# Tanh for the compression MLP's activation, and a strict alternation of MLP tiles with gate half blocks on TensorE

## The chip, the cores and the metric

The kernel runs on one core of a Trainium2 chip. The metric is the device time of one execution in microseconds (us). The engines are named as the profile names them: PE is TensorE (matmul), PEld its weight load, DVE VectorE, ACT ScalarE, POOL GpSimd, SP the engine that here only issues DMAs.

## The reference

One decoder layer over 1024 tokens of 1024 channels, in float32. What matters here is the token compression of its sparse attention branch, and the gate paths:

```
def compress_blocks(t, pe, w1, w2):      # overlapping blocks of 32 tokens, stride 16: 63 blocks
    blk = t[:, :, idx] + pe
    flat = blk.reshape(B, G, nc, CMP_BLOCK * dh)          # 2048 values a block
    return jax.nn.silu(flat @ w1) @ w2                    # hidden 256, out 64
...
proj = h @ w_in[l]                       # q, k, v, z_a, z_b, merge ... are columns of it
kc = compress_blocks(kc_raw, pe_k, w_cmp_k1, w_cmp_k2)
vc = compress_blocks(vc_raw, pe_v, w_cmp_v1, w_cmp_v2)
...
y_a = (merge_heads(o_a) * jax.nn.silu(z_a)) @ w_o_nsa
y_b = (merge_heads(o_b) * jax.nn.silu(z_b)) @ w_o_swa
```

`silu(u)` is `u / (1 + exp(-u))`, which is also `0.5 * u * (1 + tanh(u / 2))`.

## The kernel before, in words

A float32 product is formed as three passes of TensorE over operands split into a high part (a rounded cast) and a low part (operand minus high part): high times high, low times high, high times low. Every weight therefore goes through four steps: a DMA into `wraw` (SP's queue), a cast to `wh` (ACT, for the first two blocks of this stage DVE, L175), a subtraction to `wl` (POOL, L182), and then the matmuls.

The program has a prologue (norms, value and key projections, up to about 92 us), the stage that is changed here (about 92 to 192 us), the attention, and the output projections. In the changed stage three streams are interleaved:

- **The gate half blocks.** `z_steps` (L573) projects six blocks of gate columns, ZB0 to ZB3, ZA0 and ZA1. A block has two token halves of 24 matmuls of 512 columns (L580, L583, L584), and is a generator that yields after each 12: 24 steps in all, each called by `z_step`. The result leaves a bank of PSUM (`b_s` and `b_pj` in turn) in `z_out`: a tanh on ACT (L569), a multiplication on DVE (L570), a store.
- **The two MLPs.** `blocks_of(side)` copies the raw keys or values into overlapping blocks `flat` with four copies on ACT (L705, the key-block copies for side 0) and adds the position embedding on DVE (L706). `mlp(side)` splits `flat` into `fh` (ACT, L714) and `fl` (DVE, L715), and walks over eight tiles of the first weight matrix, each with a load to `w1raw` (ACT's queue), a cast (ACT, L722), a subtraction (DVE, L723) and six matmuls of 256 columns (L726, L729, L730). Then come the activation (`he`, L735 to L738), two transposes on PE (L741), the copy `h1T` (L743), and the second matrix (L749 or L760).
- **Side work hung on the gate steps.** `gate_sum` loads 16 rows `gr` of the modulation weights (ACT's queue, L670, two buffers) and reduces each on DVE (L672). `input_sums` forms sums of the normed input on POOL (L634, L637). When the last `gr` is reduced, the same buffer takes the distance table `DC`, which the first attention scores need (L925).

The order on each engine is made by a scheduler that follows priorities and the extra orderings given by `after(ins, other)`, which add no wait of their own, only a place in the order. Each engine then runs its list strictly in order; an instruction that waits holds up everything behind it. `last["act"]` and `last["dve"]` are the ACT and the DVE instruction of the last query block of the prologue (`q_block`, L522 and L523). `z_done[-1]` is the last matmul of the newest gate step.

Before, the tiles of an MLP are ordered behind gate steps only in part (L727), the gate steps are not ordered behind MLP tiles at all, and no gate step is called between the end of `mlp(0)` and the second tile of `mlp(1)`.

Of the kernel before, what the change touches and what calls it, by code (L numbers as in the profile page):

```python
# [7 lines left out]
F32 = mybir.dt.float32  # L8
F32R = mybir.dt.float32r
AF = mybir.ActivationFunctionType  # L10
ALU = mybir.AluOpType
# [3 lines left out]
P = 128  # L15
# [55 lines left out]
def hybrid_kernel(tc, io, out):  # L71
# [97 lines left out]
    def split_half(raw, shape, low=None):  # L169
        wh = wp.tile(shape, F32R, name="wh", tag="wh", bufs=WBUFS)  # L170
        wl = wp.tile(shape, F32R, name="wl", tag="wl", bufs=WBUFS)
        if low is None and hold[0] is None and not ended:
            cast_count[0] += 1
            if cast_count[0] < 3:
                after(ins := nc.vector.tensor_copy(wh, raw), last["dve"])  # L175
            else:
                after(ins := nc.scalar.copy(wh, raw), last["act"])
        else:
            ins = nc.scalar.copy(wh, raw)  # L179
        chain("wh", ins)  # L180
        if low is None:
            chain("wl", nc.gpsimd.tensor_tensor(wl, raw, wh.bitcast(F32), ALU.subtract))  # L182
        else:
            act(ins)
            low.append(lambda: chain("wl", dve(nc.vector.tensor_tensor(wl, raw, wh.bitcast(F32), ALU.subtract))))
        return wh, wl
# [386 lines left out]
    def z_steps(names):  # L573
        w = load_block(names[0])
        for n, name in enumerate(names):
            for half in range(2):
                t = bank(("s", "pj")[z_count[0] % 2])
                for kc in range(KC):
                    wh, wl = (x[:, kc % KH, :] for x in w[kc // KH])
                    ins = nc.tensor.matmul(t, lhsT=wh, rhs=hh[kc][half], start=(kc == 0), stop=False)  # L580
                    if kc == 0:
                        chain("pj", ins)
                    nc.tensor.matmul(t, lhsT=wh, rhs=hl[kc][half], start=False, stop=False)  # L583
                    ins = nc.tensor.matmul(t, lhsT=wl, rhs=hh[kc][half], start=False, stop=(kc == KC - 1))  # L584
                    if kc == 3:
                        yield ins
                z_out(name, half, t)
                if half == 0 and n + 1 < len(names):
                    following = load_block(names[n + 1])
                yield ins  # L590
            w = following
# [91 lines left out]
    with tc.tile_pool(name="c1", bufs=1, reuse_waits="tile") as c1:  # L683
# [12 lines left out]
        def blocks_of(side):  # L696
            raw = raws[side]
            pe = sm.tile([P, 16], F32, name="pe", tag="pe", bufs=2)
            after(nc.scalar.dma_start(pe, io["peT"][side]), last["act"])
            flat = c1.tile([P, 16, P], F32, name="flat", tag="flat", bufs=1)  # L700
            nc.gpsimd.memset(flat[:, :, 126:], 0.0)
            for g in range(2):
                rg = raw[64 * g : 64 * g + 64]
                for j in range(2):
                    nc.scalar.copy(flat[64 * j : 64 * j + 64, :, 63 * g : 63 * g + 63], rg[:, :, j : j + 63])  # L705
            nc.vector.tensor_tensor(  # L706
                flat[:, :, :126], flat[:, :, :126], pe.unsqueeze(2).broadcast_to([P, 16, 126]), ALU.add)
            flats.append(flat)

        def mlp(side):  # L710
            flat = flats[side]
            fh = c1.tile([P, 16, P], F32R, name="fh", tag="fh", bufs=1)
            fl = c1.tile([P, 16, P], F32R, name="fl", tag="fl", bufs=1)
            nc.scalar.copy(fh, flat)  # L714
            nc.vector.tensor_tensor(fl, flat, fh.bitcast(F32), ALU.subtract)  # L715
            t = bank("pt")
            for n in range(8):
                raw = c1.tile([P, HS], F32, name="w1raw", tag="w1raw", bufs=3)
                chain("w1raw", nc.scalar.dma_start(raw, io["w1"][side, n]))

                w1h, w1l = (kq.tile([P, P + HS], F32R, name="w1", tag="kts", bufs=8)[:, :HS] for _ in range(2))
                chain("kts", nc.scalar.copy(w1h, raw))  # L722
                nc.vector.tensor_tensor(w1l, raw, w1h.bitcast(F32), ALU.subtract)  # L723
                for l in (2 * n, 2 * n + 1):
                    h, lo = (x[:, l % 2 * 256 : l % 2 * 256 + 256] for x in (w1h, w1l))
                    ins = nc.tensor.matmul(t[:, :256], lhsT=fh[:, l, :], rhs=h, start=(l == 0), stop=False)  # L726
                    if n and (side == 0 or n % 2 == 0) and l == 2 * n:  # L727
                        after(ins, z_done[-1])
                    nc.tensor.matmul(t[:, :256], lhsT=fh[:, l, :], rhs=lo, start=False, stop=False)  # L729
                    nc.tensor.matmul(t[:, :256], lhsT=fl[:, l, :], rhs=h, start=False, stop=(l == 15))  # L730
                if (side == 0 or n % 2) and n < 7:
                    with tc.high_priority(offset=-500):
                        z_step()
            he = c1.tile([P, 256], F32, name="he", tag="he", bufs=1)
            nc.scalar.activation(he[:126], t[:126, :256], AF.Exp, scale=-1.0)  # L735
            nc.vector.tensor_scalar(he[:126], he[:126], 1.0, None, ALU.add)
            nc.vector.reciprocal(he[:126], he[:126])
            nc.vector.tensor_tensor(he[:126], t[:126, :256], he[:126], ALU.mult)  # L738
            t = bank("pt")
            for k in range(2):  # L740
                nc.tensor.transpose(t[:, k * P : k * P + 126], he[:126, k * P : k * P + P], ident[:126, :126])  # L741
            h1T = c1.tile([P, 2, 126], F32, name="h1T", tag="h1T", bufs=1)
            nc.vector.tensor_copy(h1T, t[:, :256].rearrange("p (k r) -> p k r", k=2)[:, :, :126])  # L743
            t = bank("pt")
            if side == 0:
                w2 = c1.tile([P, 2, P], F32, name="w2k", tag="w2")
                nc.scalar.dma_start(w2, io["w2k"])
                for k in range(2):
                    nc.tensor.matmul(t[:, :126], lhsT=w2[:, k, :], rhs=h1T[:, k, :], start=(k == 0), stop=(k == 1))  # L749
                kcf = c1.tile([P, 2, 64], F32, name="kcf", tag="cf", bufs=2)  # L750
                nc.vector.memset(kcf, 0.0)
                nc.vector.tensor_copy(kcf[:, :, :63], t[:, :126].rearrange("p (g c) -> p g c", g=2))
                nc.vector.tensor_copy(kc2[:, 0], kcf)
                nc.vector.tensor_tensor(kc2[:, 1], kcf, kc2[:, 0].bitcast(F32), ALU.subtract)
            else:
                w2 = c1.tile([P, 2, 64], F32, name="w2v", tag="w2")
                nc.scalar.dma_start(w2, io["w2v"])
                for g in range(2):
                    for k in range(2):
                        nc.tensor.matmul(  # L760
                            t[:63, g * 64 : g * 64 + 64], lhsT=h1T[:, k, 63 * g : 63 * g + 63], rhs=w2[:, k, :],
                            start=(k == 0), stop=(k == 1))

                for par in range(2):
# [5 lines left out]
                    nc.vector.tensor_tensor(vc2[:, par, :, 1, :], vcf, vc2[:, par, :, 0, :].bitcast(F32), ALU.subtract)  # L770


        zs = z_steps([f"Z{m}{b}" for m, b in (("B", 0), ("B", 1), ("B", 2), ("B", 3), ("A", 0), ("A", 1))])
        for _ in range(3):
            z_step()
        with tc.high_priority(offset=500):
            blocks_of(0)
            mlp(0)
            blocks_of(1)
            mlp(1)  # L780
        while len(z_done) < 24:
            z_step()
        for n in sorted(z_work):
# [1006 lines left out]
```

## Time and profile before

| what | value |
|---|---|
| time, median of 3 runs | 893.46 us (892.33 to 894.55) |
| the profiled execution: time, span | 894.23 us, 892.4 us |
| mean granted TensorE clock | 0.992 |
| busy share of the span: PE, PEld, DVE, ACT, POOL | 97%, 82%, 69%, 60%, 59% |
| chain that ended last | PE through the output stage, then a tail on DVE, ACT and POOL |
| window 92 to 192 us: PE busy, granted clock | 88.05 us of 100, 0.95 |
| window 192 to 250 us: PE busy, granted clock | 58.00 us of 58, 1.00 |

The span runs from the first to the last instruction; the time of the execution is about 2 us longer. A matmul of 512 columns shows a length of about 0.39 us, but matmuls overlap: what counts for the length of a stretch is the distance of their starts. An idle time in square brackets is that of the engine just before the instruction, with what released it.

### The profile page before, as it was taken

The page shows a single profiled execution, that of the slowest core. Times are in us where ns is not written, and L with a number is a line of the kernel's source. Part 1 is how long each engine was busy: PE and PEld are TensorE (multiplying, and loading weights), DVE is VectorE, ACT ScalarE, POOL GpSimd, SP SyncE. Part 2 cuts the span into 40 slices and gives each one's busy share as a digit, 9 for nine tenths or more (in the row PEclk, how much of TensorE's full clock was granted, in tenths as well). Part 3 has the DMA queues.
Part 4 walks back from the last instruction along what each step waited for, and adds up shares of the span by engine and source line. Part 5 has one row for each costly group of instructions (what it writes and reads, how often), then busy time and mean ns, then how long its engine had stood idle before and what let it go on. Part 6 is the DMA issues. An engine that isn't in the chain of part 4 may idle for free. (4 is left out here: it accounts for less than half of the span.)

```text
span 892.4 us, 14782 instructions
## 1 busy us (share of the span) xinstructions
PE 868.3 (97%) x4418; PEld 731.9 (82%) x4418; DVE 619.0 (69%) x1587; ACT 536.2 (60%) x1220; POOL 530.3 (59%) x547
## 2 busy tenths in 40 slices
PE   9999897999999999999999999999999999999996
PEld 7889686778888888888888888888888788877885
DVE  5866756456666677766766577777676399778996
ACT  6566732247777787766656797666665475444341
POOL 1000674467878787888535597765656379645541
PEclk9999999999999999999999999999999999999998
DMA  9975495585555535474324243343363599841333
GB/s 351 308 254 155 149 313 196 158 262 177 171 145 161 154 114 180 160 242 137 91 83 144 73 133 119 113 124 107 122 192 126 158 338 300 283 129 48 107 97 116
DMA packets 93298, 151.47 MB, mean 170 GB/s; under 512 B 10913, under 2 KB 28705, under 8 KB 93218
## 3 DMA queue, kind: packets, MB, share of 16 engines
q1 hardware_dynamic: 87168, 140.38, 48.2%
q10 hardware_dynamic: 6050, 10.14, 3.9%
q8 instruction: 35, 0.57, 0.3%
q14 instruction: 45, 0.37, 0.1%
HBM read 108.81 MB, written 38.01 MB: 165 GB/s over the span
## 5 line engine op out<-in xcount | busy, mean ns | idle before, releaser
L182 POOL TENSOR_TENSOR wl<-wraw,wh 128x512 fp32r<-128x512 f32 x123 | 164.3, 1339 | 110.6 <-ACT wh L179 66.7
L991 DVE TENSOR_TENSOR pl<-b_pt,ph 128x512 fp32r<-128x512 f32 x162 | 110.7, 687 | 39.1 <-ACT ph L990 38.2
L990 ACT CAST ph<-b_pt 128x512 fp32r<-128x512 f32 x162 | 93.5, 584 | 55.6 <-PE b_pt L984 46.6
L938 ACT ACTIVATE ps<-ps,mins 128x257 f32<-128x257 f32 (+9 forms) x128 | 81.3, 636 | 37.3 <-DVE mins L925 29.9
L179 ACT CAST wh<-wraw 128x512 fp32r<-128x512 f32 x115 | 70.6, 618 | 54.3 <-PE b_pj L1063 18.0
L915 PE MATMUL b_s<-kh,q 128*128 128x256 f32 (+6 forms) x272 | 86.0, 322 | 2.1 <-DVE sp L570 1.6
L918 PE MATMUL b_s<-kl,q 128*128 128x256 f32 (+6 forms) x272 | 83.5, 314 | 0.0
L947 POOL TENSOR_SCALAR ps<-ps,rr,gates 128x128 f32<-128x128 f32 (+7 forms) x64 | 52.4, 822 | 50.5 <-DVE rr L942 31.6
L1058 PE MATMUL b_pj<-hh,wh 128*128 128x512 f32 x188 | 77.4, 412 | 0.0
L1064 PE MATMUL b_pj<-hh,wl 128*128 128x512 f32 x188 | 74.0, 394 | 0.0
L1063 PE MATMUL b_pj<-hl,wh 128*128 128x512 f32 x188 | 74.0, 394 | 0.0
L995 PE MATMUL b_pv<-pl,V 128*128 128x512 f32 x162 | 68.3, 422 | 1.2 <-DVE pl L991 0.9
L984 PE MATMUL b_pt<-ident,ps 128*128 128x128 f32 x408 | 67.1, 272 | 0.0
L992 PE MATMUL b_pv<-ph,V 128*128 128x512 f32 x162 | 66.7, 412 | 0.1
L915 PEld LDWEIGHTS b_s<-kh,q 128*128 128x128 f32 x272 | 51.2, 188 | 9.9 <-DVE sp L570 1.8
L984 PEld LDWEIGHTS b_pt<-ident,ps 128*128 128x128 f32 x408 | 51.0, 140 | 9.2
L947 POOL TENSOR_SCALAR pw<-pw,rr,gates 128x640 f32<-128x640 f32 (+4 forms) x64 | 47.3, 742 | 17.9 <-DVE rr L942 10.8
L918 PEld LDWEIGHTS b_s<-kl,q 128*128 128x128 f32 x272 | 51.2, 189 | 7.2
L938 ACT ACTIVATE pw<-pw,mins 128x640 f32<-128x640 f32 (+4 forms) x64 | 44.5, 696 | 11.9 <-DVE mins L925 11.0
L942 DVE RECIPROCAL rr<-sums 128x1 f32<-128x1 f32 x192 | 28.2, 159 | 28.1 <-ACT pw L938 13.3
L925 DVE CUSTOM_DVE_ANT_0 ps<-b_s,DC 128x512 f32<-128x512 f32 (+3 forms) x64 | 35.0, 553 | 13.8 <-PE b_pt L984 10.2
L205 PE MATMUL b_pj<-hh,wh 128*128 128x512 f32 x112 | 44.5, 397 | 0.0
(463 smaller groups left out, 2581.1 us busy)
## 6 DMA issues: line engine op xcount, KB each, us to landing
wraw<-in_w_blk SPq DMA_DIRECT2D x83, 256.0 KB, 3.2
r<-in_w_out SPq DMA_DIRECT2D x32, 256.0 KB, 4.8
wa<-in_w_adaT SPq DMA_DIRECT2D x15, 512.0 KB, 4.6
wraw<-sS SPq DMA_DIRECT2D x28, 256.0 KB, 2.8
w1raw<-in_w ACTq DMA_DIRECT2D x16, 256.0 KB, 2.7
gr<-in_w_adaT ACTq DMA_DIRECT2D x16, 256.0 KB, 4.3
wraw<-in_w_o SPq DMA_DIRECT2D x16, 256.0 KB, 4.3
t<-od SPq DMA_DIRECT2D x16, 256.0 KB, 4.7
```

Of the source, the lines that this page charges most:

```text
L179: ins = nc.scalar.copy(wh, raw)
L182: chain("wl", nc.gpsimd.tensor_tensor(wl, raw, wh.bitcast(F32), ALU.subtract))
L915: ins = nc.tensor.matmul(sp[:, :n_in], lhsT=q, rhs=rh, start=True, stop=False)
L918: nc.tensor.matmul(sp[:, :n_in], lhsT=q, rhs=rl, start=False, stop=True)
L938: nc.scalar.activation(rows[r][:, :on], rows[r][:, :on], AF.Exp, scale=-1.0, bias=last_min[:, r : r + 1], accum_out=sums[:, r : r + 1])
L947: nc.gpsimd.tensor_scalar(rows[r][:, :off], rows[r][:, :off], rr[:, r : r + 1], gate, ALU.mult, ALU.mult)
L984: ins = nc.tensor.transpose(t[:, r * P : r * P + P], rows[r][:, off : off + P], ident)
L990: nc.scalar.copy(ph, t)
L991: nc.vector.tensor_tensor(pl, t, ph.bitcast(F32), ALU.subtract)
L1058: ins = nc.tensor.matmul(self.t, lhsT=wh[:, kc, :], rhs=hi, start=(self.first is None and kc == 0), stop=False)
L1063: nc.tensor.matmul(self.t, lhsT=wh[:, kc, :], rhs=lo, start=False, stop=False)
L1064: ins = nc.tensor.matmul(self.t, lhsT=wl[:, kc, :], rhs=hi, start=False, stop=(kc == KH - 1 and self.stop))
```

## The change

1. The activation of the MLP is `tanh(u/2)` on ACT and one `(tanh + 1) * u` on DVE, in place of exp on ACT and add, reciprocal and multiply on DVE. The factor 0.5 is taken with the copy `h1T`, which becomes a multiplication.
2. Every MLP tile is ordered behind the newest gate step, and every gate step (12 matmuls) behind the newest MLP tile and the gate half before it. A gate step is called behind each of the 16 tiles, and one more behind each MLP's activation.
3. The end of an MLP (transposes, `h1T`, second matrix) becomes a generator of two parts. That of side 0 runs behind the second and third tile of side 1; that of side 1 behind two more gate steps.
4. The four block copies and the position's addition are ordered behind the last query's instruction on ACT (`last["act"]`) and behind DVE's first two weight casts (`last["cast"]`, which later is the activation of the first MLP). The second side's blocks are called within the first MLP (behind its third tile).
5. `fh` and `fl` are formed in two halves.

```diff
@@ split_half
             if cast_count[0] < 3:
                 after(ins := nc.vector.tensor_copy(wh, raw), last["dve"])
+                last["cast"] = ins
@@ z_steps
+                    if kc in (0, 4):
+                        for earlier in ("mlp", "z"):
+                            if earlier in last:
+                                after(ins, last[earlier])
...
+                last["z"] = ins
                 z_out(name, half, t)
@@ blocks_of
-                    nc.scalar.copy(flat[...], rg[:, :, j : j + 63])
-            nc.vector.tensor_tensor(flat..., pe..., ALU.add)
+                    ins = nc.scalar.copy(flat[...], rg[:, :, j : j + 63])
+                    after(ins, last["act"])
+            ins = nc.vector.tensor_tensor(flat..., pe..., ALU.add)
+            after(ins, last["cast"])
@@ mlp
-            nc.scalar.copy(fh, flat)
-            nc.vector.tensor_tensor(fl, flat, fh.bitcast(F32), ALU.subtract)
+            for part in (slice(0, 8), slice(8, 16)):
+                nc.scalar.copy(fh[:, part], flat[:, part])
+                ins = nc.vector.tensor_tensor(fl[:, part], flat[:, part], fh[:, part].bitcast(F32), ALU.subtract)
+                after(ins, last["cast"])
...
-                    if n and (side == 0 or n % 2 == 0) and l == 2 * n:
+                    if l == 2 * n:
                         after(ins, z_done[-1])
...
-                if (side == 0 or n % 2) and n < 7:
-                    with tc.high_priority(offset=-500):
-                        z_step()
+                if side == 0 and n == 2:
+                    blocks_of(1)
+                if side and n in (1, 2):
+                    next(ends_[0])
+                with tc.high_priority(offset=-500):
+                    z_step()
...
-            nc.scalar.activation(he[:126], t[:126, :256], AF.Exp, scale=-1.0)
-            nc.vector.tensor_scalar(he[:126], he[:126], 1.0, None, ALU.add)
-            nc.vector.reciprocal(he[:126], he[:126])
-            nc.vector.tensor_tensor(he[:126], t[:126, :256], he[:126], ALU.mult)
+            nc.scalar.activation(he[:126], t[:126, :256], AF.Tanh, scale=0.5)
+            last["cast"] = nc.vector.scalar_tensor_tensor(he[:126], he[:126], 1.0, t[:126, :256], ALU.add, ALU.mult)
+            with tc.high_priority(offset=-500):
+                z_step()
+            ends_.append(mlp_end(side, he))
...
-            nc.vector.tensor_copy(h1T, t[:, :256]...)
+            nc.vector.tensor_scalar(h1T, t[:, :256]..., 0.5, None, ALU.mult)
+            yield
@@ the calls
             blocks_of(0)
             mlp(0)
-            blocks_of(1)
             mlp(1)
+            next(ends_[1])
+        z_step()
+        next(ends_[1])
         while len(z_done) < 24:
             z_step()
```

How this moves instructions is seen in the order on each engine. Line numbers behind the change are larger: L705 becomes L711, L522 becomes L523, L714 becomes L723, L741 becomes L758, L735 becomes L749, L580 becomes L581.

First, ACT where the prologue ends (`w` is a part of an MLP weight tile, `q` the last query, `flat` the blocks, `gates` and `cg` side work). Before:

```order
L722 CAST w_1248<-w1raw 128x512
L705 COPY flat<-craw 64x16x63 x4
L522 ACTIVATE q<-b_pt 64x512
L699 DMA pe<-in_peT 128x16
L719 DMA w1raw<-in_w 128x512
L699 DMA pe<-in_peT 128x16
L719 DMA w1raw<-in_w 128x512
L270 ACT_TABLE_LOAD
L270 ACTIVATE gates<-gates 128x96 x2
L690 COPY craw<-b_s 128x16x32
L177 CAST wh<-wraw 128x512
L714 CAST fh<-flat 128x2048
```

And now:

```order
L732 CAST w_1259<-w1raw 128x512
L523 ACTIVATE q<-b_pt 64x512
L705 DMA pe<-in_peT 128x16
L711 COPY flat<-craw 64x16x63 x4
L705 DMA pe<-in_peT 128x16
L729 DMA w1raw<-in_w 128x512 x2
L271 ACT_TABLE_LOAD
L271 ACTIVATE gates<-gates 128x96 x2
L178 CAST wh<-wraw 128x512
L696 COPY craw<-b_s 128x16x32
L663 DMA cg<-in_c 128x512
L676 DMA gr<-in_w_adaT 128x512
```

The query now stands ahead of the four copies, and `fh` (its rows come four rows further down) behind the load `cg` and its copy.

Second, DVE at the end of the first MLP (`he` is the activation, `fl` the low part of the second MLP's blocks, the ISA rows on `gr` the reductions). Before:

```order
L570 SCALAR_TENSOR_TENSOR sp<-sp,b_s 128x512
L736 TENSOR_SCALAR he<-he 126x256
L672 ISA gr,mod<-gr,b_s,gpart 128x512
L672 ISA mod 128x1
L737 RECIPROCAL he<-he 126x256
L715 TENSOR_TENSOR fl<-flat,fh 128x2048
L723 TENSOR_TENSOR w_1493<-w1raw,w_1492 128x512
L738 TENSOR_TENSOR he<-b_pt,he 126x256
```

And now:

```order
L571 SCALAR_TENSOR_TENSOR sp<-sp,b_s 128x512
L750 SCALAR_TENSOR_TENSOR he<-he,b_pt 126x256
L724 TENSOR_TENSOR fl<-flat,fh 128x1024
L678 ISA gr,mod<-gr,b_s,gpart 128x512
L678 ISA mod 128x1
L724 TENSOR_TENSOR fl<-flat,fh 128x1024
L733 TENSOR_TENSOR w_1582<-w1raw,w_1581 128x512
```

Five rows lay between the first and the last DVE operation of the activation, its reciprocal among them; now one row is the whole of DVE's part, and the first half of `fl` follows at once.

Third, PE at the transposes of the first MLP (`b_pj` and `b_s` hold gate halves, `b_pt` the MLP). Before:

```order
L580 MATMUL b_pj<-hh_101,wh 128x512
L583 MATMUL b_pj<-hl_117,wh 128x512
L584 MATMUL b_pj<-hh_101,wl 128x512
L580 MATMUL b_s<-hh_86,wh 128x512
L741 MATMUL b_pt<-ident,he 128x126 x2
L583 MATMUL b_s<-hl_102,wh 128x512
L584 MATMUL b_s<-hh_86,wl 128x512
```

And now:

```order
L736 MATMUL b_pt<-w_1493,fh 128x256
L739 MATMUL b_pt<-w_1494,fh 128x256
L740 MATMUL b_pt<-w_1493,fl 128x256
L758 MATMUL b_pt<-ident,he 128x126 x2
L581 MATMUL b_s<-hh_94,wh 128x512
L588 MATMUL b_s<-hl_110,wh 128x512
L589 MATMUL b_s<-hh_94,wl 128x512
```

The transposes stood behind two gate halves (48 matmuls, and two more) that follow the last tile of the first MLP. Now they stand behind 24 gate matmuls, the first tile of the second MLP, 12 gate matmuls and its second tile. Those of the second MLP now stand behind 24 gate matmuls and four of the first scores, where 12 gate matmuls stood.

More of the change, by code (lines that the diff above doesn't have):

```diff
@@ L704, in blocks_of @@
                 for j in range(2):
-                    nc.scalar.copy(flat[64 * j : 64 * j + 64, :, 63 * g : 63 * g + 63], rg[:, :, j : j + 63])
-            nc.vector.tensor_tensor(
+                    ins = nc.scalar.copy(flat[64 * j : 64 * j + 64, :, 63 * g : 63 * g + 63], rg[:, :, j : j + 63])
+                    after(ins, last["act"])
+            ins = nc.vector.tensor_tensor(
                 flat[:, :, :126], flat[:, :, :126], pe.unsqueeze(2).broadcast_to([P, 16, 126]), ALU.add)
+            after(ins, last["cast"])
             flats.append(flat)
@@ L726, in mlp @@
                     ins = nc.tensor.matmul(t[:, :256], lhsT=fh[:, l, :], rhs=h, start=(l == 0), stop=False)
-                    if n and (side == 0 or n % 2 == 0) and l == 2 * n:
+                    if l == 2 * n:
                         after(ins, z_done[-1])
                     nc.tensor.matmul(t[:, :256], lhsT=fh[:, l, :], rhs=lo, start=False, stop=False)
-                    nc.tensor.matmul(t[:, :256], lhsT=fl[:, l, :], rhs=h, start=False, stop=(l == 15))
-                if (side == 0 or n % 2) and n < 7:
-                    with tc.high_priority(offset=-500):
-                        z_step()
@@ L734, in mlp @@
-            he = c1.tile([P, 256], F32, name="he", tag="he", bufs=1)
[L735 to L738, printed above, removed]
+                    last["mlp"] = nc.tensor.matmul(
+                        t[:, :256], lhsT=fl[:, l, :], rhs=h, start=False, stop=(l == 15))
@@ L739, in mlp, with mlp_end @@
+            with tc.high_priority(offset=-500):
+                z_step()
+            ends_.append(mlp_end(side, he))
+        def mlp_end(side, he):
             t = bank("pt")
             for k in range(2):
-                nc.tensor.transpose(t[:, k * P : k * P + 126], he[:126, k * P : k * P + P], ident[:126, :126])
+                ins = nc.tensor.transpose(t[:, k * P : k * P + 126], he[:126, k * P : k * P + P], ident[:126, :126])
+                after(ins, z_done[-1])
             h1T = c1.tile([P, 2, 126], F32, name="h1T", tag="h1T", bufs=1)
-            nc.vector.tensor_copy(h1T, t[:, :256].rearrange("p (k r) -> p k r", k=2)[:, :, :126])
@@ L744, in mlp @@
-            t = bank("pt")
+            nc.vector.tensor_scalar(
+                h1T, t[:, :256].rearrange("p (k r) -> p k r", k=2)[:, :, :126], 0.5, None, ALU.mult)
+            yield
+            t = t[:, 256:]
             if side == 0:
@@ L748, in mlp @@
                 for k in range(2):
-                    nc.tensor.matmul(t[:, :126], lhsT=w2[:, k, :], rhs=h1T[:, k, :], start=(k == 0), stop=(k == 1))
+                    ins = nc.tensor.matmul(
+                        t[:, :126], lhsT=w2[:, k, :], rhs=h1T[:, k, :], start=(k == 0), stop=(k == 1))
+                    after(ins, z_done[-1])
                 kcf = c1.tile([P, 2, 64], F32, name="kcf", tag="cf", bufs=2)
@@ L759, in mlp @@
                     for k in range(2):
-                        nc.tensor.matmul(
+                        ins = nc.tensor.matmul(
                             t[:63, g * 64 : g * 64 + 64], lhsT=h1T[:, k, 63 * g : 63 * g + 63], rhs=w2[:, k, :],
                             start=(k == 0), stop=(k == 1))
+                        after(ins, z_done[-1])
                 for par in range(2):
@@ L770, in mlp @@
                     nc.vector.tensor_tensor(vc2[:, par, :, 1, :], vcf, vc2[:, par, :, 0, :].bitcast(F32), ALU.subtract)
+            yield
+        ends_ = []
         zs = z_steps([f"Z{m}{b}" for m, b in (("B", 0), ("B", 1), ("B", 2), ("B", 3), ("A", 0), ("A", 1))])
```

## The prediction

> **What bounds the kernel now.** I read the busy times first, then the stretches between stages, then who waited for whom on PE, and last the order in time around each wait.
>
> ```profile
> PE 868.3 (97%) x4418; PEld 731.9 (82%) x4418; DVE 619.0 (69%) x1587; ACT 536.2 (60%) x1220; POOL 530.3 (59%) x547
> ```
> ```profile
> 92.00:192.00 100.00, 88.05 (x421) 73.16 (x420) 58.47 (x96) 37.08 (x63) 60.98 (x43) 0.95 0.66 213
> 192.00:250.00 58.00, 58.00 (x314) 49.50 (x314) 35.11 (x108) 43.38 (x123) 47.27 (x59) 1.00 0.58 187
> ```
> ```profile
> PE b_pt L741 <- DVE he L738: 6.6, 2, 4.9
> ...
> PE b_s L915 <- DVE sp L570: 1.6, 1, 1.6
> ```
>
> The second fence gives stretches: start and end, length, busy time of PE, PEld, DVE, ACT and POOL, granted clock, DMA share, GB/s. PE is the bound: outside the changed stage it hardly idles (58.00 of 58 behind it). Inside it idles 100 - 88.05 = 11.95 us, and the clock of 0.95 costs another 0.05 x 88 = 4.4 us. The third fence (the longest waits of PE in the whole run: waiter, releaser, us in all, times, longest) puts nearly all of that idle time in four places. In order of time, PE there (start, length, idle before, releaser):
>
> ```profile
> 96.38 0.77 PE L580 MATMUL b_s<-hh,wh 128*128 128x512 f32 x1 [3.57 <-DVE wh L175]
> 104.74 0.28 PE L730 MATMUL b_pt<-w,fl 128*128 128x256 f32 x1
> 126.72 0.28 PE L726 MATMUL b_pt<-w,fh 128*128 128x256 f32 x1
> 127.43 0.40 PE L580 MATMUL b_s<-hh,wh 128*128 128x512 f32 x1
> 130.89 0.40 PE L580 MATMUL b_pj<-hh,wh 128*128 128x512 f32 x1
> 142.03 0.39 PE L580 MATMUL b_s<-hh,wh 128*128 128x512 f32 x1
> 147.28 0.68 PE L741 MATMUL b_pt<-ident,he 126*128 126x126 f32 x2 [4.87 <-DVE he L738]
> 150.59 0.39 PE L584 MATMUL b_s<-hh,wl 128*128 128x512 f32 x1
> 178.53 0.44 PE L741 MATMUL b_pt<-ident,he 126*128 126x126 f32 x2 [1.77 <-DVE he L738]
> 181.16 0.80 PE L580 MATMUL b_pj<-hh,wh 128*128 128x512 f32 x1 [0.16 <-DVE sp L570]
> 184.64 0.40 PE L584 MATMUL b_pj<-hh,wl 128*128 128x512 f32 x1
> ```
>
> The undisturbed pace comes from 130.89 to 142.03: 49 gate matmuls in 11.14 us, 0.227 each. A tile of six MLP matmuls takes 127.43 - 126.72 = 0.71. So a gate step with its tile is 12 x 0.227 + 0.71 = 3.44 us. After each gap the matmuls run slow: 8 take 3.21 us from 96.38 (at pace 1.82: 1.39 lost); the two transposes and 7 gate matmuls take 3.31 from 147.28 (about 1.9 at pace: 1.4 lost); 8 take 3.48 from 181.16 (1.66 lost). Idle 3.57 + 4.87 + 1.77 + 1.59 + 0.16 = 11.96, slow matmuls 4.4: **16.4 us** are to be had, and no more.
>
> **The change part by part.** No matmul is added or removed, so a gain is a gap that closes.
>
> *The first gap.* PE waits for the cast `wh`, and this is why (ACT, DVE, POOL; the L714 row gives shortest, median and longest of its two, in ns):
>
> ```profile
> 88.56 1.04 ACT L705 COPY flat<-craw 64x1008 f32<-64x1008 f32 x1
> 92.80 0.59 ACT L522 ACTIVATE q<-b_pt 64x512 fp32r<-64x512 f32 x1
> 88.11 1.29 DVE L723 TENSOR_TENSOR w<-w1raw,w 128x512 fp32r<-128x512 f32 x2
> 92.81 2.26 DVE L706 TENSOR_TENSOR flat<-flat,pe 128x2016 f32<-128x2016 f32 x1 [3.41 <-ACT flat L705]
> 95.10 0.69 DVE L523 SCALAR_TENSOR_TENSOR q<-b_pt,q 64x512 fp32r<-64x512 f32 x1
> 95.81 0.76 DVE L175 CAST wh<-wraw 128x512 fp32r<-128x512 f32 x2
> L714 ACT CAST fh<-flat x2: 1902/1903/1904, 96.2 to 137.8; 128x2048 fp32r<-128x2048 f32 x2
> 96.32 3.88 POOL L182 TENSOR_TENSOR wl<-wraw,wh 128x512 fp32r<-128x512 f32 x3 [25.34 <-DVE wh L175]
> 96.49 2.53 DVE L271 TENSOR_SCALAR gates<-gates 128x96 f32<-128x96 f32 x2
> 98.94 1.35 DVE L272 RECIPROCAL gates<-gates 128x96 f32<-128x96 f32 x2
> 100.21 2.22 DVE L715 TENSOR_TENSOR fl<-flat,fh 128x2048 fp32r<-128x2048 f32 x1
> 102.36 1.25 DVE L276 TENSOR_SCALAR gates<-gates,smalls 128x8 f32<-128x8 f32 x1
> ```
>
> Four copies hold the last query on ACT until 92.80, and the position's addition holds DVE until 95.1. With the query first, ACT has it done at 88.56 + 0.59 = 89.2; DVE ends L723 at 89.4, the query's low part at 90.1, the casts at 90.8. POOL's first subtraction (3.88 / 3 = 1.29) starts at 90.6 and ends at 91.9, the next at 93.2. SP's next weight load, which that subtraction frees, moves ahead with it. PE comes free at 96.38 - 3.57 = 92.8 and needs the second half of the block 12 x 0.227 later, at 95.5. Nothing is late: 3.57 + 1.39 are gained.
>
> What is late next is the blocks, now 0.6 later. PE runs 36 gate matmuls (8.2 us) to 101.0 before the first tile, and 0.24 later wants half of `fl`. On DVE: copies end at 89.2 + 4.2 = 93.4, addition 95.7, gates 2.53 + 1.35 + 1.25 to 100.8 (L276 now stands ahead of `fl`), half of `fl` 1.11 to 101.9: PE waits 0.7. `fh` is not later: the copy of `cg` ahead of it needs a load issued at about 93; with 4.3 us to landing (the median of the like loads `gr`, below), some 0.6 for the copy and half of 1.90 for half of `fh`, it is done at 98.9. Bounds: 0, if the gates run faster, and 2.4, if `fl` takes the slower time seen (3.13, below, a half of it 1.57) behind one more POOL operation of 1.29. I take 1.0.
>
> Here a rule of the Trainium skill bears on a row. L715 takes 2.22 us once and 3.13 us once, L736 0.295 and 1.308 in the row below. The Trainium skill, "SBUF — State Buffer", section "Who interferes with whom", says that a VectorE operation with two SBUF inputs blocks against a GpSimd operation that reads SBUF, for a whole instruction. By that, two halves of `fl` can meet two POOL operations instead of one, which speaks against this edit: the wait would be about 2.3 us and the sum below 1.3 smaller. By the rows alone it is 1.0.
>
> *The second gap.* The end of the first MLP (ACT, then DVE; the L736 row as the L714 row above):
>
> ```profile
> 137.50 0.38 ACT L735 ACTIVATE he<-b_pt 126x256 f32<-126x256 f32 x1 [0.31 <-issue]
> L736 DVE TENSOR_SCALAR he<-he x2: 295/802/1308, 137.9 to 174.5; 126x256 f32<-126x256 f32 x2
> 139.75 0.75 DVE L672 CUSTOM_DVE_ANT_0 gr<-gr,b_s,gpart 128x512 f32<-128x512 f32 x1 [1.55 <-DMA gr<-in_w_adaT]
> 140.43 1.75 DVE L737 RECIPROCAL he<-he 126x256 f32<-126x256 f32 x1
> 142.09 3.13 DVE L715 TENSOR_TENSOR fl<-flat,fh 128x2048 fp32r<-128x2048 f32 x1
> 146.82 0.41 DVE L738 TENSOR_TENSOR he<-b_pt,he 126x256 f32<-126x256 f32 x1
> ```
>
> The last tile ends at 130.9, `he` at 147.2, 16.3 us later; PE passes 50 gate matmuls (11.4 us) and waits. Now DVE's part is one operation (like L738, 0.41, for 0.3 to 1.3 + 1.75 + 0.41), directly behind the tanh (0.38, as the exp). Even if ACT is as late as here (137.5 - 130.9 = 6.6 us), `he` is done 7.4 us behind the last tile; the transposes come 24 + 12 gate matmuls and two tiles behind it, 9.6 us. The wait is gone: 4.87 + 1.4.
>
> But the second MLP's first tile now comes 24 x 0.227 = 5.45 us behind the first's last, and 0.24 later wants half of `fl`. That needs ACT's lag, 0.38 for the tanh, 0.95 for half of `fh`, and 1.1 to 1.6 on DVE. With a lag of 6.6 that makes 9.3 against 5.7, a new wait of 3.6 us, and 1.4 of slow matmuls with it. What sets the lag? ACT's queue holds the loads of `gr`, each waiting for the reduction two before it, and each reduction waits for its load:
>
> ```profile
> 109.54 0.75 DVE L672 CUSTOM_DVE_ANT_0 gr<-gr,b_pv,smalls 128x512 f32<-128x512 f32 x1
> 119.09 0.73 DVE L672 CUSTOM_DVE_ANT_0 gr<-gr,b_pv,smalls 128x512 f32<-128x512 f32 x1
> DMA to landing us min/median/max: 2.6/4.3/6.1
> ```
>
> From the third reduction (119.09) to the ninth (139.75) one takes 3.44 us, PE's own step, so the lag is what it was at the start. At the start the first reduction came at 109.5, behind the second side's addition; now it stands behind the halves of `fl`, at about 103.5, with the first tile done at about 102.7 (104.9 before, by the L730 row). That is a lag of about 1 instead of 4.7, so ACT should be near 3 late, not 6.6, and the wait near 0. Between 0 and 5.0 I take 1.0, nearer the earlier start.
>
> *The third gap.* The second transposes now stand behind 24 gate matmuls and four scores (6.0 us) instead of 12, with `he` done some 1 us plus the lag behind the tile: 1.77 is gone. The 1.59 and 0.16 were `sp` queued behind the reciprocal on DVE, which is gone too, and so are the 1.66 of slow matmuls. The second matrix of each MLP stands 4 us or more behind its transposes, and `h1T` (0.4 either way) needs only that DVE isn't held by a `gr` load: 0, at most 1.
>
> *At no cost:* two more casts and two more subtractions from the halves; DVE is busy 58 of 100 us, ACT 37. The tanh is in the same function table as the gates' (ACT runs both before, with no table load between). POOL's sums move with the gate steps: 61 us of work in a stage of now about 85.
>
> *The sum:* 16.4 - 1.0 - 1.0 = **14.4 us**. The attention's order changes slightly behind the stage; with PE at 58.00 of 58 there I give it 0, and 1 either way. The profiled execution took 894.23 us (span 892.4), 0.77 above the median of 893.46. So 894.23 - 14.4 = 879.8 for that one, and 893.46 - 14.4 = 879.1 for a median.
>
> **The rivals.**
>
> *The lag stays.* ACT and DVE keep their 6.6 us, and the second MLP's first tile waits 3.6 with 1.4 of slow matmuls behind it; the first tile waits up to its 2.4. Gain 16.4 - 5.0 - 1.7 = 9.7, time about 883.8. For it: the lag was steady for six steps. Against it: the earlier start.
>
> *No change.* The gain is lost at the door of the attention. Its first score operation needs `DC`, which is loaded behind the last reduction:
>
> ```profile
> 183.12 0.75 DVE L672 CUSTOM_DVE_ANT_0 gr<-gr,b_s,gpart 128x512 f32<-128x512 f32 x1 [1.03 <-DMA gr<-in_w_adaT]
> 183.96 0.33 ACTq L804 DMA_DIRECT2D DC<-in_DC  x1
> 189.51 0.35 DVE L925 CUSTOM_DVE_ANT_0 ps<-b_s,DC,nsink 128x128 f32<-128x128 f32 x1
> ```
>
> That load takes up to 5.5 us; if the reductions still ended at 183.9, the scores' banks would fill and PE would wait until 189.5 as before: about 893. PE will want it at about 172, so the ninth reduction (now about 132) and seven more must take over 4.9 us each before this costs anything. Against it: 3.44 was measured.
>
> *Slower.* The same transfers in 85 instead of 100 us land later; each MLP subtraction stands behind a reduction on DVE, so PE's step becomes half the loop of load and reduction. A landing of about 5.7 gives the 3.44. To lose 14.4 us beyond the 7 us by which the tiles are prepared ahead, 15 steps must each take 1.43 more: a landing above 8.6, where the longest was 6.1. At 9.5 the kernel takes about 900.
>
> **How the numbers follow.** The measurement cannot tell less than about 0.3% (2.7 us) from no change. Forecast (about 876 to 882): 0.67. The lag stays (882 to 888): 0.22. No change: 0.06. Slower: 0.05. The range reaches from all 16.4 gained and 1 us more from the order behind it, 876, through the second case, whose worst bounds (2.4 + 5.0 + 1 lost) give 885.5, to 887 with half a microsecond more from the `h1T`: it leaves out about 0.15. Faster by over 0.3% (below 890.8): 0.90, with a little of the third case; within: 0.05; slower (above 896.1): 0.05.
>
> **What would show it.** PE's waits at `he` (L758) and at the casts L175 gone; granted clock 1.00 nearly throughout the stage; the last gate matmul near 174 instead of 189; a wait of about 1 us at the first tile (L740, for `fl`). Wrong would be: a wait at the second MLP's first tile above 2 us (the lag), first scores waiting for `DC`, or PE waiting every step for an MLP subtraction.

## The result, and the profile after

The changed kernel takes 883.57 us in the median of 4 runs (882.20 to 884.92) against 892.89 us for the kernel before in the same session: a ratio of 0.9895, 95% interval 0.9871 to 0.9919. In a second session, in the run `c_after` below, the ratio was 0.9916 (0.9897 to 0.9935). So it is some 8 to 9 us faster. The forecast was 879.1 with a range of 876 to 887; the time lies in the range, at the figure of the rival "the lag stays" (883.8).

The profiled execution took 884.92 us (span 883.1). The page's line of busy times, the stretches of the stage and behind it (columns as in the prediction), and PE's waits:

```profile
PE 864.6 (98%) x4418; PEld 729.5 (83%) x4418; DVE 616.1 (70%) x1585; ACT 536.9 (61%) x1222; POOL 532.6 (60%) x547
```
```profile
92.00:182.00 90.00, 86.76 (x430) 72.68 (x429) 55.43 (x94) 39.84 (x68) 62.51 (x43) 0.98 0.72 247
182.00:240.00 58.00, 58.00 (x314) 49.49 (x313) 34.18 (x104) 42.96 (x119) 47.51 (x60) 1.00 0.57 179
```
```profile
PE b_pt L740 <- DVE fl L724: 2.4, 2, 1.6
PE b_pv L352 <- POOL xr L406: 1.8, 1, 1.8
...
PE b_pt L736 <- ACT fh L723: 0.8, 1, 0.8
```

PE idles 3.24 us in the stage instead of 11.95, and no wait for `he`, for the casts of L175 or for `sp` is left there. The waits that took their place are at the first tile of each MLP. PE in order of time:

```profile
94.19 0.39 PE L581 MATMUL b_s<-hh,wh 128*128 128x512 f32 x1
104.38 0.39 PE L740 MATMUL b_pt<-w,fl 128*128 128x256 f32 x1 [1.64 <-DVE fl L724]
129.06 0.28 PE L740 MATMUL b_pt<-w,fl 128*128 128x256 f32 x1
135.65 0.38 PE L736 MATMUL b_pt<-w,fh 128*128 128x256 f32 x1 [0.84 <-ACT fh L723]
136.91 0.39 PE L740 MATMUL b_pt<-w,fl 128*128 128x256 f32 x1 [0.76 <-DVE fl L724]
138.35 0.63 PE L581 MATMUL b_s<-hh,wh 128*128 128x512 f32 x1
140.91 0.61 PE L581 MATMUL b_s<-hh,wh 128*128 128x512 f32 x1
142.55 0.38 PE L758 MATMUL b_pt<-ident,he 126*128 126x126 f32 x2
179.19 0.39 PE L589 MATMUL b_pj<-hh,wl 128*128 128x512 f32 x1
```

The gate blocks start at 94.19 with nothing idle before them. Between 138.35 and 140.91 six gate matmuls take 2.56 us, 0.427 each where 0.227 is the pace: the slow matmuls behind a wait, eight of them in all, 1.6 us. Both pairs of transposes run without a wait.

Where the 9.3 us between the two profiled executions come from is read from three marks: the end of the prologue, the first matmul of the attention's last projections (tile `hht`; the rows give shortest, median and longest in ns, first and last start), and the end. Before, then after:

```profile
L1058 PE MATMUL b_pj<-hht,wh x80: 387/396/477, 536.1 to 689.1; 128*128 128x512 f32 x80
```
```profile
L1085 PE MATMUL b_pj<-hht,wh x80: 387/397/477, 527.5 to 680.5; 128*128 128x512 f32 x80
```

Prologue: 92.8 before, 94.2 after, 1.4 us longer. From there to the mark: 443.3 before, 433.3 after, **10.0 us shorter**. Behind it: 358.1 and 357.4, 0.7 shorter. The sum is -9.3, the difference of the two times (894.23 and 884.92). The prologue's 1.4 us are no effect of the change: the same kernel shows either length (tanh alone, below: its gate blocks wanted to start at 92.7 in one execution and 94.1 in another; with the whole change and one more gate step, `e4_step`, they start at 92.4). The first 20 us, before and after:

```profile
0.00:20.00 20.00, 18.52 (x74) 14.95 (x75) 10.24 (x27) 13.63 (x23) 4.40 (x12) 1.00 0.92 353
```
```profile
0.00:20.00 20.00, 15.77 (x65) 12.70 (x66) 9.82 (x26) 12.23 (x21) 4.42 (x12) 0.83 0.92 358
```

So of the 14.4 us that were forecast, 10.0 came in this pair of executions. The last gate matmul starts at 179.2, where the prediction named about 174.

### The profile page after: what moved, and what is told of

Same layout as the page of the kernel before. It is cut to its first block, busy times and chain, and to the rows that moved or that the text cites. A ratio compares the mean times of both kernels' runs of the same rounds, so it can differ in the third digit from the quotient of the medians.

```text
span 883.1 us, 14777 instructions
## 1 busy us (share of the span) xinstructions
PE 864.6 (98%) x4418; PEld 729.5 (83%) x4418; DVE 616.1 (70%) x1585; ACT 536.9 (61%) x1222; POOL 532.6 (60%) x547
## 4 chain that ended last, share of the span: by engine, by line
PE 88%; DVE 4%; DMA 3%; ACT 2%; issue 1%; POOL 1%; SPq 0%; ACTq 0%; DVEq 0%; POOLq 0%
PE b_pt L1011 8%; PE b_pj L1085 7%; PE b_pj L1091 7%; PE b_pj L1090 7%; PE b_s L945 4%; PE b_pv L1022 4%; PE b_s L942 4%; PE b_pv L1019 4%; PE b_pj L213 3%; PE b_pj L206 3%; PE b_pj L214 3%; PE b_s L1460 1%; PE b_s L1458 1%; PE b_s L1459 1%; PE b_s L229 1%
## 5 line engine op out<-in xcount | busy, mean ns | idle before, releaser
L183 POOL TENSOR_TENSOR wl<-wraw,wh 128x512 fp32r<-128x512 f32 x123 | 166.5, 1357 | 92.2 <-ACT wh L180 68.6
L1085 PE MATMUL b_pj<-hh,wh 128*128 128x512 f32 x188 | 77.4, 412 | 0.0
L1090 PE MATMUL b_pj<-hl,wh 128*128 128x512 f32 x188 | 74.0, 393 | 0.0
L213 PE MATMUL b_pj<-hl,wh 128*128 128x512 f32 x112 | 44.2, 395 | 0.0
```

The source lines that it names most:

```text
L1085: ins = nc.tensor.matmul(self.t, lhsT=wh[:, kc, :], rhs=hi, start=(self.first is None and kc == 0), stop=False)
L1090: nc.tensor.matmul(self.t, lhsT=wh[:, kc, :], rhs=lo, start=False, stop=False)
```

## The experiments

All times are medians; the ratio is to the kernel before on the same chip. "Order" stands for edits 2, 3 and 5 and for the earlier call of the second side's blocks; tanh and order without the copies was not run.

| kernel | copies | tanh | order | us | ratio (95%) |
|---|---|---|---|---|---|
| `e1_copies` | yes | | | 888.78 | 0.9944 (0.9925 to 0.9964) |
| `e2_tanh` | | yes | | 893.34 | 0.9995 (0.9974 to 1.0015) |
| `e7_order` | | | yes | 894.79 | 1.0015 (0.9994 to 1.0036) |
| `e8_noorder` | yes | yes | | 888.29 | 0.9949 (0.9931 to 0.9968) |
| `e3_exp` | yes | | yes | 887.35 | 0.9932 (0.9911 to 0.9953) |
| `c_after` | yes | yes | yes | 885.48 | 0.9916 (0.9897 to 0.9935) |
| `e4_step` | yes | yes | one step more | 881.09 | 0.9866 (0.9846 to 0.9886) |

### One edit at a time

**The copies alone** (`e1_copies`): the kernel before with

```diff
-                    nc.scalar.copy(flat[...], rg[...])
+                    ins = nc.scalar.copy(flat[...], rg[...])
+                    after(ins, last["act"])
...
+            after(ins, last["cast"])
```

> The kernel before with edit 4 alone (the four block copies behind the last query on ACT, the position's addition behind DVE's two weight casts); activation, order of tiles and gate steps, and the blocks' two parts as before. Theory A (each gap has its own price): the first gap of 3.57 us and its 1.39 us of slow matmuls go, a wait of 0 to 2 us for fl comes at the first MLP tile, the second and third gaps stay as long as they were: 3 to 5 us less than before, about 889. Theory B (what holds he is a loop of loads and reductions that does not start earlier): the time won at the first gap is given back at the transposes, whose wait grows from 4.9 to about 8 us: 893, no change. The wait of PE for he in the trace tells them apart.

888.78 us, 5 less. Theory A holds on the time, and PE's waits show how:

```profile
PE b_pt L744 <- DVE he L741: 5.0, 2, 3.2
```

The first gap is gone (the first gate matmul starts at 93.60). The transposes' wait did not grow, it fell from 4.9 to 3.2, and no wait for `fl` came at the first tile. This is the one edit that pays by itself.

**The tanh alone** (`e2_tanh`): the kernel before with the `he` and `h1T` lines of the change.

> The kernel before with edit 1 alone (tanh and one DVE operation in place of exp, add, reciprocal and multiply; the factor 0.5 with h1T). Theory A (the DVE part of the activation makes the second and third gaps): he is done about 8 us earlier, at about 139, and the transposes do not wait; 4.87 + 1.4 us go, and of the third gap's 1.77 + 1.59 + 0.16 + 1.66 us at least half: 8 to 11.4 us less, about 883, nearly what the whole change gives. The first gap of 3.57 us stays. Theory B (the order, not the activation, makes the gaps): PE still waits for he 3 us or more, and the time is above 889.

893.34 us, no change, which neither theory had. Its profiled execution was its fastest (889.29), so a second one was profiled.

> The kernel before with the tanh alone, a second profile, since the first came from its fastest execution (889.3 against a median of 893.3). Theory A (in the old order the waits of the stage depend on when each gr load lands, and the first profile shows a lucky one): a slower execution, 892 to 895, with waits for he, h1T or sp in the stage that are 3 to 5 us longer than in the first. Theory B (the spread has nothing to do with the stage): the same waits in the stage, and the time lost elsewhere.

893.43 us. PE's waits in the first execution, then in the second:

```profile
PE b_s L914 <- DVE sp L570: 1.4, 1, 1.4
...
PE b_pt L739 <- DVE he L736: 0.8, 1, 0.8
...
PE b_pt L748 <- DVE h1T L741: 0.6, 1, 0.6
```
```profile
PE b_s L914 <- DVE sp L570: 1.9, 1, 1.9
...
PE b_pt L739 <- DVE he L736: 0.9, 1, 0.9
PE b_pt L748 <- DVE h1T L741: 0.8, 1, 0.8
```

The wait for `he` is short in both: the DVE chain did make that gap. But a wait for `h1T` stands behind it, and the first scores still wait for `sp`. The waits are alike within 0.5 us each; the 4.1 us between the executions lie in the prologue (1.3) and in slow matmuls. Stretches 97 to 140 and 160 to 190, first and second execution; the columns are as above, with the granted clock next behind POOL:

```profile
97.00:140.00 43.00, 42.18 (x202) 35.27 (x201) 28.44 (x39) 19.82 (x30) 32.70 (x24) 0.96 0.79 266
160.00:190.00 30.00, 27.25 (x130) 22.50 (x129) 12.74 (x37) 8.55 (x22) 19.18 (x15) 0.94 0.76 254
```
```profile
97.00:140.00 43.00, 41.77 (x193) 34.87 (x193) 27.95 (x39) 18.88 (x30) 33.26 (x23) 0.93 0.77 250
160.00:190.00 30.00, 27.05 (x120) 22.06 (x119) 11.64 (x34) 8.04 (x19) 19.20 (x15) 0.89 0.72 239
```

Theory A of that run fell (no wait of the stage was 3 to 5 us longer), and B holds in part: the same waits, but with more or fewer slow matmuls behind them, within the stage. Since each kernel has one or two profiles and its executions spread by 1.5 to 9 us (before: 888.75 to 897.97 in 26 runs), how the tanh's shorter waits and its unchanged median go together in every execution stays open.

**The order alone** (`e7_order`): the changed kernel with exp and with the copies as before.

> The changed kernel without edits 1 and 4: the alternation, the later ends of the MLPs and the halves of fh and fl, but with the old activation by exp and with the copies ordered as before. Theory A: the first gap stays (5.0 us); the second and third gaps close, because the transposes stand behind more work; but the halves of the second fl stand behind the reciprocal and the multiplication, so the second MLP's first tile waits 4 to 5 us with 1.7 us of slow matmuls: about 5 us less than before, 888. Theory B (order and activation do the same work twice, either is enough): the transposes' wait is gone and fl is no later than in the changed kernel: about 885.

894.79 us, no gain, where theory A had 888. It had the mechanism and half of its size:

```profile
PE b_pt L738 <- DVE fl L721: 6.6, 1, 6.6
...
PE b_pt L734 <- ACT fh L720: 2.0, 1, 2.0
```

The transposes no longer wait, but the second MLP's first tile does, 8.6 us with 2 us of slow matmuls: the wait for `he` was turned into one for `fl`, which stands behind the reciprocal and the multiplication on DVE.

**Two of three.** Copies and order with the old activation (`e3_exp`):

> The changed kernel with the old activation (exp, add, reciprocal, multiply; h1T a plain copy), everything else as changed. Theory A (the tanh is worth what it takes from DVE ahead of the second fl): the waits at the second MLP's first tile grow from 1.6 us by 0.3 to 1.3 + 1.75 + 0.7 us, 3 to 4 us more: about 887. Theory B (the new order hides the activation wholly, the tanh was not needed): within 1 us of the changed kernel, 883 to 884.5.

887.35 us, as theory A had it. The waits at the second MLP's first tile are 1.4 + 3.4 instead of 0.8 + 0.8 us. Behind the new order the tanh is worth about 3 us (from the first gate matmul to the projections this trace is 3.5 us longer than the change's; the medians differ by 1.9 on the same chip, and the two intervals overlap); there the short chain on DVE counts because `fl` follows it.

Copies and tanh in the old order (`e8_noorder`):

> The kernel before with edits 1 and 4 together (tanh, and copies behind the last query), the order of tiles and gate steps and the two parts of fh and fl as before. Theory A (the effects of single edits add up as the gaps do): without the first gap (4.9 us) and with the second and third gaps as short as in the profile of the tanh alone (5.4 us left of 11.4), 5 + 6 = 11 us less than before, about 882.5: the new order would not be needed. Theory B (in the old order the tanh's gain does not last: its median was 893.3, though one execution took 889.3): only the copies count, 888 to 889, and the order is worth 5 us.

888.29 us, theory B: within the error of the copies alone. So each of the tanh and the order gains nothing by itself, and little on top of the copies; only both, on top of the copies, give the whole.

### What holds the second MLP's first tile

**The change once more, and one more gate step** (12 matmuls) between the MLPs (`c_after`, `e4_step`):

```diff
             mlp(0)
+            with tc.high_priority(offset=-500):
+                z_step()
             mlp(1)
```

> The changed kernel once more, as the measure for the three others on this chip. Both theories: 883 to 884, with waits of 1.6 us at the first MLP tile and of 0.8 + 0.8 us and 1.7 us of slow matmuls at the second MLP's first tile, as in its first profile.

885.48 us, 1.5 more than expected; waits of 1.68 at the first tile and 0.79 + 1.75 at the second MLP's. The first half of `fl` took 2.22 us there, behind a sum that POOL had begun 0.13 us before it; in the first profile the two began together, `fl` took 1.23 us and POOL's sum 2.38.

> The changed kernel with one more gate step (12 matmuls, 2.7 us) between the two MLPs. Theory A (the second MLP's first tile waits only because ACT and DVE are some 5 us behind PE there): its two waits of 0.84 + 0.76 us and the 1.7 us of slow matmuls behind them go: 3 to 3.5 us less than the changed kernel, about 880. Theory B (what holds the halves of fh and fl is the chain of loads and reductions, which keeps pace with the gate steps): the wait stays, within 1 us of the changed kernel.

881.09 us, 4.4 less than the change on the same chip; the two intervals do not overlap. The wait at the second MLP's first tile is gone, and one for `h1T` is new:

```profile
PE b_pt L740 <- DVE fl L724: 1.7, 1, 1.7
PE b_pt L769 <- DVE h1T L761: 1.7, 1, 1.7
```

From the first gate matmul to the projections the two traces differ by only 1.2 us. The prologue was 1.7 us shorter here and the part behind the mark 2.2 longer, and the profiled execution was the slowest of four. How much of the 4.4 us is the step's, and how much the prologue's, stays open.

**One step more ahead of the first tile too** (`e6_both`: as `e4_step`, with four calls of `z_step` instead of three ahead of `blocks_of(0)`):

> The changed kernel with one more gate step between the MLPs and one more ahead of the first MLP tile (36 + 12 matmuls stand before it). Theory A: both waits go, 1.8 us more than with the step between the MLPs alone: about 878.3, 5 us less than the changed kernel. Rival: no gate matmuls are left to stand between the second MLP's last tile, its transposes and its second matrix, so that a wait for he or h1T of 2 to 5 us appears there: 880 to 883.

889.04 us (0.9961, 0.9946 to 0.9976): both expectations fell. The first tile's wait is gone, but that of the second MLP is back, 1.6 for `fh` and 1.6 for `fl`, though the same 36 gate matmuls stand ahead of it. Eleven loads of `gr` now stand ahead of `he` on ACT, where ten do in the change and in `e4_step`:

```profile
136.62 0.34 ACTq L676 DMA_DIRECT2D gr<-in_w_adaT  x1
137.00 0.38 ACT L749 ACTIVATE he<-b_pt 126x256 f32<-126x256 f32 x1 [3.01 <-PE b_s L589]
137.28 1.98 ACT L723 CAST fh<-flat 128x1024 fp32r<-128x1024 f32 x2
```

ACT idles 3 us until that load is issued; the releaser named is a matmul into `b_s`, which `he` does not read. The reduction that frees the load's buffer had ended at 133.9. The trace's semaphore events (a semaphore is a counter by which a transfer or an engine tells that it is done), which these rows leave out, show the wait: the issue waited until 136.54 for the landing of a load of `w1raw` issued at 130.50, which raises the same semaphore as this `gr` load (the last section has the same in the changed kernel).

**The gr loads issued by SP** (`e9_grsp`: `nc.scalar.dma_start` becomes `nc.sync.dma_start` in `gate_sum`):

> The changed kernel with the loads of gr issued by SP instead of ACT; the order of the matmuls is the same, and the halves of the second fh now stand ahead of the tanh of he on ACT. Theory A (the second MLP's first tile waits because ACT's in-order queue holds he and fh behind a gr load that itself waits for a reduction): fh no longer waits 5 us, the waits of 0.8 + 0.8 us (0.8 + 1.8 in the second profile) and their 1.7 us of slow matmuls go: 3 to 4 us less than the changed kernel, ratio to before about 0.987, 881 to 882. Theory B (the wait moves with the loads): SP holds the loads of the gate weights behind gr instead, and PE waits for wh or wl of a gate step: no gain, 884 or more.

886.62 us (0.9935, 0.9912 to 0.9959), no gain, theory B's figure without its mechanism. `fh` is free of the loads, and PE waits 3.5 us for `fl` all the same:

```profile
131.34 1.99 ACT L723 CAST fh<-flat 128x1024 fp32r<-128x1024 f32 x2
133.22 0.38 ACT L749 ACTIVATE he<-b_pt 126x256 f32<-126x256 f32 x1
134.73 0.75 DVE L678 CUSTOM_DVE_ANT_0 gr<-gr,b_s,gpart 128x512 f32<-128x512 f32 x1 [2.56 <-DMA gr<-in_w_adaT]
135.40 0.42 DVE L750 SCALAR_TENSOR_TENSOR he<-he,b_pt 126x256 f32<-126x256 f32 x1
135.73 3.54 DVE L724 TENSOR_TENSOR fl<-flat,fh 128x1024 fp32r<-128x1024 f32 x2
```

Freed on ACT, the wait went over to DVE, whose queue holds `he` and `fl` behind a reduction that waits for its load. The loop of loads and reductions holds both engines.

### What holds the first tile

**The gates' operations behind gate step 19**, on top of the step more (`e10_gates`: `form_gates(0)` and `form_gates(1)` called at mark 19 in place of ahead of the stage):

> The changed kernel with one more gate step between the MLPs (as in the run with that step alone) and with the attention gates' operations on ACT and DVE moved from ahead of the first fl to behind gate step 19. Theory A (DVE's 5.2 us for the gates, from the position's addition to fl, make the wait of 1.7 us at the first MLP tile): fl is ready some 5 us earlier, that wait goes, nothing else moves: 1.5 to 2 us less than with the step alone, about 879, ratio to before 0.984. Theory B (as with one more step ahead of the first tile, all that follows comes earlier on PE and the loop of gr does not, so the wait comes back at the second MLP): 881 or more.

880.75 us (0.9866, 0.9840 to 0.9892), the same as with the step alone; the wait at the first tile is 1.55 us, so theory A fell, and the wait at the second MLP that theory B named did not come. ACT, then DVE:

```profile
92.55 0.34 ACTq L663 DMA_DIRECT2D cg<-in_c  x1
98.62 0.59 ACT L667 COPY b_pv<-cg 128x512 f32<-128x512 f32 x1 [3.51 <-DMA cg<-in_c]
99.15 1.99 ACT L725 CAST fh<-flat 128x1024 fp32r<-128x1024 f32 x2
```
```profile
100.23 2.17 DVE L726 TENSOR_TENSOR fl<-flat,fh 128x1024 fp32r<-128x1024 f32 x1 [3.82 <-ACT fh L725]
```

With DVE free, `fl` waits for `fh`, and `fh` for the copy of `cg`, whose load took 6 us. Counted from the first gate matmul (92.34 here, 94.19 in the change) `fl` starts 7.9 us in where it was 8.9, but PE waits only 0.1 less. The first half took 2.17 us, beside a POOL operation that ran from 100.02 to 101.32, against 1.21 in the change.

**All three** (`e11_all`: step, gates, SP):

> All three: one more gate step between the MLPs, the gates' operations behind gate step 19, and the gr loads issued by SP. Theory A (two causes, DVE's queue at the first tile and ACT's queue at the second MLP): no wait of PE above 0.5 us left in the stage but for h1T, 878 to 879. Theory B (SP then holds the gate weights): waits for wh or wl, 882 or more.

883.73 us (0.9907, 0.9879 to 0.9936), by theory B's figure, but not by its mechanism: PE waits 1.5 us at the first tile and 2.7 at the second MLP's, again for `fl`, which stands behind a reduction on DVE; no gate step waits for `wh` or `wl`. In the median it is 3 us slower than without the move to SP, but the two intervals overlap.

## Why the prediction was right or wrong

- **The first gap** closed as worked out: 4.96 us, and `e1_copies` shows the copies as its cause (4.7 us less).
- **The first tile's wait** was taken at 1.0 and was 1.64 (1.8 with slow matmuls), between the 0 and 2.4 of its bounds. The term that was short is the position's addition: it took longer than its row of before, and so the gates' operations ended later on DVE (the last row is the first half of `fl`):

```profile
94.87 4.56 POOL L640 TENSOR_TENSOR q<-hh,hl 128x512 f32<-128x512 f32 x2
95.17 3.11 DVE L713 TENSOR_TENSOR flat<-flat,pe 128x2016 f32<-128x2016 f32 x1 [2.66 <-ACT flat L711]
101.94 1.26 DVE L277 TENSOR_SCALAR gates<-gates,smalls 128x8 f32<-128x8 f32 x1
103.12 1.21 DVE L724 TENSOR_TENSOR fl<-flat,fh 128x1024 fp32r<-128x1024 f32 x1
```

  Before, the addition took 2.26 us with POOL idle; here POOL works beside it and it takes 3.11, so that the gates are done at 103.2 and the first half of `fl` starts then. The 0.85 us are nearly all of what the working's 0.7 lacked; the first half of `fl` took 1.21 where 1.11 was put. `e10_gates` shows that `fh` and its `cg` load were hardly earlier. The Trainium skill, "SBUF — State Buffer", section "Who interferes with whom", has DVE operations with two SBUF inputs and GpSimd reads exclude each other for a whole instruction; these rows agree with it. By that rule the wait was put at 2.3, by the rows of before at 1.0; 1.64 lies between.
- **The second gap** closed for `he`, as worked out: 6.27 us. What the prediction got wrong is the lag behind it. It let ACT's lag fall from 6.6 to near 3 us because the first reduction would come early. The last tile of the first MLP ended at 129.2 and the tanh began at 134.28, a lag of 5.1. The step that failed is "now it stands behind the halves of `fl`": it followed the first reduction only. The second side's addition, which stood ahead of the first reduction, now stands behind the second, and with it the loop pauses (DVE, and ACT in the last two rows):

```profile
107.86 0.74 DVE L678 CUSTOM_DVE_ANT_0 gr<-gr,b_pv,smalls 128x512 f32<-128x512 f32 x1
110.85 2.26 DVE L713 TENSOR_TENSOR flat<-flat,pe 128x2016 f32<-128x2016 f32 x1 [2.24 <-ACT flat L711]
116.44 0.73 DVE L678 CUSTOM_DVE_ANT_0 gr<-gr,b_pv,smalls 128x512 f32<-128x512 f32 x1
133.12 0.74 DVE L678 CUSTOM_DVE_ANT_0 gr<-gr,b_pv,smalls 128x512 f32<-128x512 f32 x1
133.90 0.33 ACTq L676 DMA_DIRECT2D gr<-in_w_adaT  x1
134.28 0.39 ACT L749 ACTIVATE he<-b_pt 126x256 f32<-126x256 f32 x1
```

  The third reduction comes at 116.44, 8.6 us behind the second, and the eighth ends at 133.86, on which the load ahead of the tanh is issued. A second thing that the prediction had not is in this lag: the load before that one was held 1.4 us (last section). Without it the eighth reduction could have started when its own load landed, at 131.99, and not at 133.12: by this estimate 1.1 us of the 5.1 are the hold's. The wait cost 1.6 us and slow matmuls 2.0, 3.6 against the 1.0 that was taken and the 5.0 of the rival. `e4_step` shows it to be a lag and no steady loss (one step more closes it), `e9_grsp` that it follows the loop when the loads leave ACT, `e6_both` that a held load can bring it back.
- **The third gap** closed: no wait for `he` or `sp` is left there. The cost of `h1T`, put at 0 to 1, was 0 in the change and 1.7 in `e4_step`, where DVE stood at a reduction waiting for its load, the condition that the prediction named.
- **The sum:** 16.4 - 1.8 - 3.6 = 11.0, against 10.0 measured up to the projections; about 1 us is lost in the attention, whose order was given 0 and 1 either way. Between the stage and the projections PE idles 1.7 us before (192 to 536) and 2.4 now (182 to 527), in short waits of at most 0.7 each; no run took that apart further. The upper end of the range, 887, is 1 us more than its own terms give (885.5 and half a microsecond).
- **The rivals.** `DC` came in time, and PE waited at no step for an MLP subtraction; "no change" and "slower" had no sign in the trace. "The lag stays" gave the time, with a smaller wait than it named (3.6 us lost for 5.0) and the attention's 1 us in its place; that the two agree within 0.3 us is luck.
- **What the prediction did not see** is that its terms are not separate: by it the tanh alone would have been worth most of the gain, and it was worth nothing measurable.

The fastest version is the change with one more gate step between the MLPs, 881.09 us (with the gates moved too, 880.75).

## What to carry to other kernels

When a reordering makes the consumer come earlier, ask what sets the pace of the producer: if it is a loop of loads and reductions in the queues of two engines, follow every instruction that moved into that loop, not only its first. More work of the bounding engine between producer and consumer closed such a wait here, until one more load came to stand ahead of it; freeing one of the two queues only moved it to the other. And an edit's worth is not additive: the copies, the tanh and the order were worth 5, 0 and 0 us alone and 8 together.

## What was not expected of the hardware

- **Whether slow matmuls follow a short wait is not told by its length.** A single wait of 1.64 (the first tile), 1.69 and 1.69 (`e4_step`) or 1.83 us (`e8_noorder`) was followed by matmuls at full pace. Waits of 0.84 and 0.76 with 0.4 us of matmuls between were followed by eight at 0.427; one of 2.73 (`e11_all`) by seven, 3.52 (`e9_grsp`) by ten. But at the first tile of `e9_grsp` waits of 0.92 and 0.75, with as much between, were followed by full pace:

```profile
102.91 0.38 PE L740 MATMUL b_pt<-w,fl 128*128 128x256 f32 x1 [0.75 <-DVE fl L724]
```

  The Trainium skill, "TensorE: Matmul & The Clock Gate", section "Why this matters for your kernels", warns of gaps above about 3 us; here 1.6 us in two pieces was enough once, and 1.67 in two pieces was not.
- **The issue of a load can wait for the landing of another load that it has nothing to do with.** In the changed kernel ACT stood 3.2 us, while the next instruction of its queue was a `gr` load:

```profile
125.91 0.33 ACTq L729 DMA_DIRECT2D w1raw<-in_w  x1
...
131.42 0.33 ACTq L676 DMA_DIRECT2D gr<-in_w_adaT  x1
131.85 0.62 ACT L732 CAST w<-w1raw 128x512 fp32r<-128x512 f32 x1 [3.16 <-DMA T1d<-q]
```

  The reduction that frees the buffer had ended at 130.03; the thirteen other loads that wait for one were issued within 0.1 us of its end, this one 1.4 us behind. The row names the store `T1d`, but that store, issued at 128.71, landed only 4.9 us later. The trace's semaphore events show the wait: this load's landing is told by a semaphore that the load of `w1raw` issued at 125.91 also raises, and the issue waited until that one had landed, at 131.35. The same semaphore held the same load by 1.7 us in `c_after`, 1.2 in `e4_step` and 2.0 in `e10_gates`.

- **The prologue's length differs by 1 to 2 us between executions**, with tanh alone in two of one kernel. Of the 14 profiled executions six have the slower one (the change, `c_after`, `e1_copies`, the second of tanh alone, `e8_noorder`, `e11_all`). In these PE does its first matmuls faster, then waits 1.4 to 1.8 us for `xr`, and the granted clock of the first 20 us is 0.74 or 0.83 instead of 1.00.
